# A retention head first, summed retention states, query decays by pieces, and work handed from VectorE to ScalarE in a fused hybrid block

## The chip, the cores and the metric

The kernel runs on one core of a Trainium2 chip. The metric is device time in microseconds (us) of one execution, lower is better. TensorE (PE in the profile) multiplies matrices, VectorE (DVE) and ScalarE (ACT) do the element-wise work, GpSimd (POOL) and SyncE (SP) mostly issue DMAs. Matrix products write to PSUM, whose banks DVE and ACT read.

## The reference

One block of a hybrid encoder over 1040 positions (16 meta tokens and 1024 inputs) of width 1024, in float32: a token mixer of four mLSTM heads and four retention heads, an output product, and a gated MLP with a causal convolution. Cut to what matters here:

```python
u = rmsnorm(h)                                   # (1040, 1024)
proj = u @ w_in                                  # q, k, v, o of 8 heads, and the gates' i, f columns
# heads 0..3, mLSTM
q, k = silu(causal_conv4(q)), silu(causal_conv4(k))
li = 15 * tanh(i / 15); lf = log_sigmoid(f)      # gates: decays between positions, from the data
h_ml = mlstm(q, k, v, li, lf)                    # state C = decay * C + k^T v, chunk by chunk
# heads 4..7, retention
q, k = rotary(q), rotary(k)                      # t1*cos - t2*sin, t1*sin + t2*cos on the two halves
h_rt = retention(q, k, v, log_gamma)             # the same state with a constant decay for each head
h += concat(sigmoid(o) * norm(h_ml), silu(g) * norm(h_rt)) @ w_out
a = causal_conv3(rmsnorm(h) @ w_up)
h += (silu(a) * (rmsnorm(h) @ w_gate)) @ w_down
out = rmsnorm(h)
```

## The kernel before

**Products.** Every product is made of three: each operand is split into a high part, rounded to a shorter format, and the low rest (`hi`, `lo`; L149 and L150 for the weights, `split` with L785 and L786 for the rest), and hi*hi, lo*hi and hi*lo are summed in PSUM (L374 to L376 for v, L384 to L386 for q, k and o, `mm3` L823 to L825 in the scan).

**Stages.** To about 38 us the input is normalised and v of the first head computed; `first_norm` gives the row scales `Rc` (positions on partitions) and `Rb` (positions along the row). Then q and k of the first head. Then the heads one after the other, some 83 us each, to about 700 us; the product with w_out to 865, the MLP's two halves to 1310 and 1545 us.

**A head.** The 1040 positions are 9 chunks, one of 16 and eight of 128. The three pieces 400, 384 and 256 wide are the groups of q, k and o. For head h the code writes, interleaved by `merge`: the six groups of o with chunks 0 to 3 of the scan; the nine groups of v of head h+1 with chunks 4 to 8 and the norms of the outputs (`post_steps`); `tables(h+1)`; the groups of q and k of head h+1. One chunk of the scan is `scan_a` (scores s, their decayed form pt, decayed keys kw, decayed queries qd) and `scan_b` (u = kw^T v, n = pt v + qd S, state C, its split S).

**mLSTM tables.** After q piece 0 of the first head, `gates()` computes decays of all four mLSTM heads with positions along the row, with small matmuls pg, pe, pf, pt in between, and writes them to the DRAM tensor `scr`. `tables(h)` loads for each head two tables spread over 128 partitions: A1 (decays within a chunk: mask added by L533, exponential by L536) and A2 (decays of queries). A1 is read by `scan_a` for pt (L803), A2 for qd (L810). Retention heads use A1 and A2 for the rotary cosines and sines instead.

**Order.** The Tile framework schedules the program: it takes the order of the code as a priority, simulates engines and queues, and sets one fixed order for each engine and each DMA queue. An engine executes its instructions in that order, so one that waits holds up all behind it; SP issues its DMAs in order too. PSUM is given out in tags: `pp` three banks, `sA` two, `num`, `upd` and `tr` one each. A PSUM bank is written again only when its readers are done.

**Other names.** `wsum` (L192, L194) prepares sums of blocks of w_out and w_down in DRAM by accumulating DMAs on POOL, one set per call of `wsum_next`. `gts` (L352) takes the gates' eight columns, which ride with v of the first head (264 columns instead of 256). `mx` (L908) is the gated, normed output, `sig` the activated o, `vl` (L350) the low part of v, whose reading frees the bank of pv.

Of the kernel before, what the change touches and what calls it, by code (L numbers as in the profile page):

```python
# [17 lines left out]
P = 128  # L18
# [21 lines left out]
R36 = NCH * H  # L40
PIECES = [(0, 400, (0, 1, 2, 3)), (400, 784, (4, 5, 6)), (784, 1040, (7, 8))]
# [12 lines left out]

V_MIX, V_FFN, V_FIN, V_MLG, V_RTG, V_CONV, V_FCONV, V_BI, V_BF = 0, 8, 16, 24, 32, 40, 72, 138, 139
V_N = 140
C_ID, C_M01, C_GV, C_GV0, C_EPS = 0, 128, 256, 260, 264
C_N = 268
# [3 lines left out]
def body(ctx, tc, h_in, vecs, cst, mask_in, rot, w_v0, w_v, w_fm, w_out, w_up, w_gate, w_down, out):  # L62
# [18 lines left out]
    cs = per.tile([P, C_N], F32, name="cs")  # L81
# [51 lines left out]
    def issue(upto):  # L133
        while issued[0] < min(upto, len(units)):
# [8 lines left out]
            sub = 2 if key[:2] == ("v", 0) else 1  # L143
# [18 lines left out]
    def u_v(h):  # L162
        for half in range(2):
            if h == 0:
                unit(("v", 0, half), w_v0[half], 4 * 264)
            else:
                unit(("v", h, half), w_v[h - 1, half], 4 * 256)
# [6 lines left out]
    def last_two(k, raw=None):  # L174
        raw = raw_tile(f"m{k}") if raw is None else raw
        nc.sync.dma_start(raw[:, :D], w_out[k])
        for t in range(2):
            if k:
# [27 lines left out]
    u_v(0)  # L206
    u_f(0, "q")
    u_f(0, "k")
    for h in range(8):
        u_f(h, "o")  # L210
        if h:
            u_m(h - 1)
        if h < 7:
            u_v(h + 1)
            u_f(h + 1, "q")
            u_f(h + 1, "k")
# [114 lines left out]
    Rg = st.tile([P, H, NCH], F32, name="Rg")  # L331
    ug = st.tile([P, KB, 32], F32, name="ug")
# [14 lines left out]
    def v_evac(h, c, L, src):  # L347
# [3 lines left out]
        if h == 0:  # L351
            nc.vector.tensor_scalar(gts[:L, :, c, :], src[:L, DV:DV + 8].rearrange("p (a b) -> p a b", a=2), Rc[:L, c:c + 1], None, ALU.mult)  # L352

    def v_group(h, c, tag="pp"):
        t0, L = CH[c]
        nv = 264 if h == 0 else 256
# [33 lines left out]
    def qk_group(h, kind, p):  # L390
# [7 lines left out]
        if h < H:  # L398
# [9 lines left out]
            nc.vector.tensor_scalar(cv[:, :n], raw[:, 3:3 + n], vec[:, w + 3:w + 4], None, ALU.mult)  # L408
            for j in (2, 1, 0):
                nc.vector.scalar_tensor_tensor(cv[:, :n], raw[:, j:j + n], vec[:, w + j:w + j + 1], cv[:, :n], ALU.mult, ALU.add)  # L410
            x = nc.scalar.activation(dst, cv[:, :n], AF.Silu)
            if h == 0 and kind == "q" and p == 0:
                after(x, last["sqrt"])
        else:
            nc.vector.tensor_tensor(raw[0:64, :n], pt[64:128, :n], A2[64:128, t0:t1], ALU.mult)
            nc.vector.tensor_tensor(raw[64:128, :n], pt[0:64, :n], A2[0:64, t0:t1], ALU.mult)
# [98 lines left out]

    def tables(h):
        if h > H:
            return
        if h == H:
            nc.sync.dma_start(A1, rot[:, 0])  # L520
            nc.sync.dma_start(A2, rot[:, 1])
            nc.vector.tensor_tensor(A2, A2, Rb, ALU.mult)
            nc.vector.tensor_tensor(A1, A1, Rb, ALU.mult)
# [253 lines left out]
    pre = {}  # L777
    state = {}
    outs = {}

    def split(src, n, nm, tag):
# [5 lines left out]
        return hi, lo  # L787

    def scan_a(h, c):
# [12 lines left out]
        if h < H:  # L802
            nc.vector.tensor_tensor(ptf[:, :L], s[:, :L], A1[:, t0:t0 + L], ALU.mult)  # L803
            if not last:
                w = cols[:, 1, c * H + h:c * H + h + 1]
                nc.scalar.activation(kh, s[:, P:2 * P], AF.Copy, scale=w)
                nc.vector.scalar_tensor_tensor(kl, s[:, P:2 * P], w, kh.bitcast(F32), ALU.mult, ALU.subtract)
# [149 lines left out]
    def first_norm(i):  # L957
# [11 lines left out]
        for f in evacs[i]:  # L969
            f()  # L970
# [37 lines left out]

# [576 lines left out]
```

## Time and profile before

| | |
|---|---|
| three runs | 1549.11, 1551.58, 1552.46 us; median 1551.58 |
| the profiled execution | 1551.16 us, its span 1549.4 us |
| PE busy | 1520.5 us, 98% of the span |
| DVE busy | 1085.4 us, 70% |
| ACT busy | 735.2 us, 47% |
| POOL busy | 90.5 us, 6% |
| DMA | 212.35 MB, 137 GB/s on average |

Matmuls overlap in the profile: one of 256 columns is shown with a duration of some 290 ns, yet the next starts 117 ns later; in full flow the start-to-start distance is 0.117 us for 256 columns and 0.175 us for 384. So busy time says little of PE's rate, and what is read are its waits (idle time before an instruction, and what released it) and the granted clock, which is 1.00 when PE runs at full speed. The page divides the span into 40 slices of 38.7 us; smaller windows are needed to see a clock that is halved for a few microseconds.

### The profile page before, as it was taken

To read this page: it belongs to the slowest core of one execution; us is meant where nothing else is said; L and a number is where in the kernel's file an instruction comes from. 1 tells how busy PE (TensorE), PEld (TensorE's weight loads), DVE (VectorE), ACT (ScalarE), POOL (GpSimd) and SP (SyncE) were. 2 spreads that over 40 slices of the span, in tenths; PEclk is the share of its full clock that TensorE was granted. 3 is DMA by queue.
4 is the path that set the end of the run, shared out by engine and by line. 5 is a ranking of instruction groups with operands and counts; after the bars stand their busy time and mean duration, and the time that the engine had idled before them with its cause. 6 is when DMAs were issued, how large, how long until landed. Compare 5 with 4: busy or idle time off the path is not lost.

```text
span 1549.4 us, 25346 instructions
## 1 busy us (share of the span) xinstructions
PE 1520.5 (98%) x9763; PEld 1398.9 (90%) x9763; DVE 1085.4 (70%) x2312; ACT 735.2 (47%) x1491; POOL 90.5 (6%) x107
## 2 busy tenths in 40 slices
PE   8989999999999999999999999999999999999997
PEld 8989999999999999997788998999999999888887
DVE  8756758686866565678867778766666666778657
ACT  7565555554242433435454455444444444434443
POOL 0110112112120210000000000000000000000000
PEclk9999999999999999999999999999999999999998
DMA  5676768778777773226542225332222224933213
GB/s 190 153 165 165 137 160 193 167 189 181 192 167 179 148 160 90 64 74 245 189 138 97 87 95 185 102 102 83 82 82 82 76 82 142 378 103 111 95 41 109
DMA packets 104904, 212.35 MB, mean 137 GB/s; under 512 B 9352, under 2 KB 31568, under 8 KB 104784
## 3 DMA queue, kind: packets, MB, share of 16 engines
q1 hardware_dynamic: 86096, 175.80, 33.9%
q0 software_dynamic: 18544, 34.87, 14.9%
q8 instruction: 76, 1.25, 0.3%
q14 instruction: 44, 0.36, 0.1%
q10 hardware_dynamic: 144, 0.07, 0.0%
HBM read 181.31 MB, written 84.19 MB: 171 GB/s over the span
## 4 chain that ended last, share of the span: by engine, by line
PE 93%; DMA 3%; DVE 2%; ACT 1%; SPq 0%; issue 0%; DVEq 0%; ACTq 0%
PE pv L374 4%; PE po L386 4%; PE po L384 4%; PE po L385 4%; PE pv L375 4%; PE pv L376 4%; PE pdx L554 3%; PE pdx L556 3%; PE pdx L555 3%; PE pup_x L555 2%; PE pup_x L556 2%; PE pga_x L554 2%; PE pga_x L556 2%; PE pga_x L555 2%; PE pup_x L554 2%; PE pk L384 2%
## 5 line engine op out<-in xcount | busy, mean ns | idle before, releaser
L374 PE MATMUL pv<-hi_v,uh 128*128 128x256 f32 (+1 forms) x512 | 148.4, 290 | 7.6 <-DVE sig L428 3.6
L375 PE MATMUL pv<-lo_v,uh 128*128 128x256 f32 (+1 forms) x512 | 147.6, 289 | 0.0
L376 PE MATMUL pv<-hi_v,ul 128*128 128x256 f32 (+1 forms) x512 | 145.8, 286 | 0.0
L384 PE MATMUL po<-uh,hi_o 128*128 128x386 f32 (+2 forms) x384 | 124.7, 325 | 0.0
L386 PE MATMUL po<-uh,lo_o 128*128 128x386 f32 (+2 forms) x384 | 122.6, 319 | 0.0
L385 PE MATMUL po<-ul,hi_o 128*128 128x386 f32 (+2 forms) x384 | 122.5, 319 | 0.0
L374 PEld LDWEIGHTS pv<-hi_v,uh 128*128 128x128 f32 x512 | 98.2, 192 | 11.6 <-DVE sig L428 3.8
L375 PEld LDWEIGHTS pv<-lo_v,uh 128*128 128x128 f32 x512 | 98.1, 192 | 0.8 <-DVE lo_v L150 0.8
L376 PEld LDWEIGHTS pv<-hi_v,ul 128*128 128x128 f32 x512 | 97.9, 192 | 0.0
L243 ACT CAST hi_up<-raw_up 128x512 fp32r<-128x512 f32 (+1 forms) x52 | 36.4, 719 | 106.7 <-PE pga_z L555 61.2
L384 PEld LDWEIGHTS po<-uh,hi_o 128*128 128x128 f32 x384 | 72.4, 188 | 0.2
L385 PEld LDWEIGHTS po<-ul,hi_o 128*128 128x128 f32 x384 | 72.4, 188 | 0.1
L386 PEld LDWEIGHTS po<-uh,lo_o 128*128 128x128 f32 x384 | 72.3, 188 | 0.0
L244 DVE TENSOR_TENSOR lo_ga<-fraw_ga,hi_ga 128x512 fp32r<-128x512 f32 (+1 forms) x52 | 41.8, 807 | 37.8 <-ACT hi_ga L243 37.6
L554 PE MATMUL pup_x<-uh_g,hi_up 128*128 128x256 f32 (+1 forms) x240 | 67.2, 282 | 0.4 <-ACT uh_g L1024 0.4
L555 PE MATMUL pup_x<-ul_g,hi_up 128*128 128x256 f32 (+1 forms) x240 | 67.4, 283 | 0.1
L244 DVE TENSOR_TENSOR lo_up<-raw_up,hi_up 128x512 fp32r<-128x512 f32 (+1 forms) x52 | 41.3, 808 | 36.0 <-ACT hi_up L243 35.2
L556 PE MATMUL pup_x<-uh_g,lo_up 128*128 128x256 f32 (+1 forms) x240 | 66.3, 282 | 0.0
L194 POOL DMA_DIRECT2D wsd<-w_down_d x55 | 50.9, 1026 | 262.8 <-DMA wsd<-w_down_d 166.1
L384 PE MATMUL pq<-uh,hi_q 128*128 128x400 f32 (+2 forms) x192 | 62.2, 324 | 3.7 <-DVE vl L350 2.5
L385 PE MATMUL pq<-ul,hi_q 128*128 128x400 f32 (+2 forms) x192 | 62.4, 325 | 0.0
L386 PE MATMUL pk<-uh,lo_k 128*128 128x400 f32 (+2 forms) x192 | 62.1, 324 | 0.0
(751 smaller groups left out, 5009.9 us busy)
## 6 DMA issues: line engine op xcount, KB each, us to landing
wsd<-w_down_d SPq DMA_DIRECT2D x22, 512.0 KB, 6.6
wsd<-w_down_d POOLq DMA_DIRECT2D x22, 512.0 KB, 6.5
raw_up<-w_up_d SPq DMA_DIRECT2D x22, 512.0 KB, 3.9
fraw_ga<-w_gate_d SPq DMA_DIRECT2D x22, 512.0 KB, 3.9
acts<-cv SPq DMA_DIRECT2D x44, 256.0 KB, 2.0
rd<-wsd SPq DMA_DIRECT2D x22, 512.0 KB, 3.3
wsd<-w_down_d POOLq DMA_DIRECT2D x33, 256.0 KB, 5.1
raw_o<-w_fm_d SPq DMA_DIRECT2D x16, 512.0 KB, 3.8
```

Source lines behind the costliest of these rows:

```text
L194: nc.gpsimd.dma_start(x, v, accum_op=ALU.add)
L243: nc.scalar.copy(hi[:, o:o + n], x)
L244: nc.vector.tensor_tensor(lo[:, o:o + n], x, hi[:, o:o + n].bitcast(F32), ALU.subtract)
L374: nc.tensor.matmul(pv[:L, :nv], a, hi[:, o:o + nv], start=kb == 0, stop=False)
L375: nc.tensor.matmul(pv[:L, :nv], a, lo[:, o:o + nv], start=False, stop=False)
L376: nc.tensor.matmul(pv[:L, :nv], b, hi[:, o:o + nv], start=False, stop=kb == KB - 1)
L384: nc.tensor.matmul(pt[:, :n], a, uh[kb][:, t0:t1], start=kb == 0, stop=False)
L385: nc.tensor.matmul(pt[:, :n], a, ul[kb][:, t0:t1], start=False, stop=False)
L386: nc.tensor.matmul(pt[:, :n], b, uh[kb][:, t0:t1], start=False, stop=kb == KB - 1)
L554: m.append(nc.tensor.matmul(pt, ah, xh_, start=first and k == 0, stop=False, skip_group_check=True))
L555: nc.tensor.matmul(pt, ah, xl_, start=False, stop=False, skip_group_check=True)
L556: m.append(nc.tensor.matmul(pt, al, xh_, start=False, stop=last and k == n - 1, skip_group_check=True))
```

## The change

It has seven parts.

1. **Order of the heads.** `ORDER = [4, 0, 1, 2, 3, 5, 6, 7]`: retention head 4 goes first, and the gates' columns ride with its v. `gates()` is written after all of the first head's q and k, no longer after q piece 0, and the mLSTM tables are first loaded for the second head in order. The rotary tables are loaded at the start (two DMAs, ahead of `raw_q` on SP) and again for head 5, since A1 and A2 are overwritten in between; their scaling by `Rb` goes by pieces (`rotary_norm`). The first head's o groups call no `wsum_next`. The first head's v scale `Rg` is computed inside `first_norm`.
2. **Summed states.** For heads 4, 5 and 6, u of all chunks accumulates in one PSUM bank, and S is split straight from it; the chunk's decay moves into the constant tables `gv` and `epsz` (new tile `gtab`), with one rescale in PSUM at chunk 4. The C instruction (L861, L865) goes for these heads. u of the next chunk now has to wait until both halves of S have been read from the bank. One DVE addition per output piece comes in for the epsilon of the norm, in all retention heads.
3. **Query decays by pieces.** mLSTM's qd is no longer computed for each of eight chunks (a product and a split each) but for three pieces, in place in A2, with the two halves in tiles of `accp`.
4. **Convolution tap.** The first of four taps, for each of the 24 groups of mLSTM's q and k, goes from DVE (L408) to ACT.
5. **Rotary moves.** The two half products (L415, L416), 64 partitions each, for the 24 groups of retention's q and k, become two ACT copies out of PSUM and one DVE product over 128 partitions.
6. **Gated output in place.** mx is written over sig, and the tile mx goes.
7. **Order of table loads.** A2's readers are done earlier because of part 3, so A2's load for the next head is issued apart from A1's.

The core of the diff:

```diff
+ORDER = [4, 0, 1, 2, 3, 5, 6, 7]
+HF = ORDER[0]
...
 def qk_group (h, kind, p)
-            nc.vector.tensor_scalar(cv[:, :n], raw[:, 3:3 + n], vec[:, w + 3:w + 4], None, ALU.mult)
+            nc.scalar.activation(cv[:, :n], raw[:, 3:3 + n], AF.Copy, scale=vec[:, w + 3:w + 4])
...
-            nc.vector.tensor_tensor(raw[0:64, :n], pt[64:128, :n], A2[64:128, t0:t1], ALU.mult)
-            nc.vector.tensor_tensor(raw[64:128, :n], pt[0:64, :n], A2[0:64, t0:t1], ALU.mult)
+            nc.scalar.copy(raw[0:64, :n], pt[64:128, :n])
+            nc.scalar.copy(raw[64:128, :n], pt[0:64, :n])
+            nc.vector.tensor_tensor(raw[:, :n], raw[:, :n], A2[:, t0:t1], ALU.mult)
             last["qk"] = nc.vector.tensor_tensor(dst, pt[:, :n], A1[:, t0:t1], ALU.mult)
             nc.vector.tensor_tensor(dst, dst, raw[:, :n], ALU.add)
...
+    def rotary_norm(t0, t1):
+        for a in (A2, A1):
+            nc.vector.tensor_tensor(a[:, t0:t1], a[:, t0:t1], Rb[:, t0:t1], ALU.mult)
...
+    def summed(h):
+        return H <= h < 7
...
 def scan_a
+            if c == max(chs[0], 1):
+                x = accp.tile([P, 2 * HB], F32R, tag=f"rr{p % 2}", name=f"qh{h}_{p}")
+                x = qds[h, p] = x[:, :p1 - p0], x[:, HB:HB + p1 - p0]
+                nc.vector.tensor_tensor(A2[:, p0:p1], qT[:, p0:p1], A2[:, p0:p1], ALU.mult)
+                nc.scalar.copy(x[0], A2[:, p0:p1])
+                nc.vector.tensor_tensor(x[1], A2[:, p0:p1], x[0].bitcast(F32), ALU.subtract)
             if c:
-                qf = wk.tile([P, P], F32, tag="qd", name=f"qd{h}_{c}", bufs=1)
-                nc.vector.tensor_tensor(qf, q, A2[:, t0:t0 + L], ALU.mult)
-                qd = split(qf, P, f"qd{h}_{c}", "qd")
+                qd = tuple(x[:, t0 - p0:t0 - p0 + L] for x in qds[h, p])
...
 def scan_b
-            up = pn[:, DV:] if one_bank else ps.tile([P, 512], F32, tag="upd", name=f"u{h}_{c}")
-            mm3(up[:, :nv], kw, v, True, True)
+            if summed(h):
+                if c == 0:
+                    state["up"] = ps.tile([P, 512], F32, tag="upd", name=f"u{h}")
+                up = state["up"]
+                if c == 4:
+                    nc.vector.tensor_scalar(up[:, :nv], up[:, :nv], float(np.exp(lg[h - H] * P * 4)), None, ALU.mult)
+            else:
+                up = pn[:, DV:] if one_bank else ps.tile([P, 512], F32, tag="upd", name=f"u{h}_{c}")
+            mm3(up[:, :nv], kw, v, not summed(h) or c == 0, True)
...
+        if c < NCH - 1 and summed(h):
+            state["S"] = split(up[:, :nv], nv, f"S{h}_{c}", "S")
...
 the program
+    tables(HF)
     for kind in "qk":
         for p in range(3):
-            qk_group(0, kind, p)
-            if kind == "q" and p == 0:
-                gates()
-    tables(0)
+            if kind == "q":
+                rotary_norm(*PIECES[p][:2])
+            qk_group(HF, kind, p)
...
+    gates()
+    for i, h in enumerate(ORDER):
-        merge([lambda b=b, p=p: (o_group(h, b, p), p == 1 and wsum_next()) for b in range(2) for p in range(3)],
+        merge([lambda b=b, p=p: (o_group(h, b, p), p == 1 and i and wsum_next()) for b in range(2) for p in range(3)],
```

Where instructions stand, at three places. The engines' rows are those of the two built programs, in the order in which each engine takes them; a name like `po0_1_1` is o of head 0, half 1, piece 1, and the last number of a name is a buffer.

DVE where the first mLSTM tables come in, in the first head's o groups, before: the mask add of A1 (L533, which waits for A1's DMA) stands between the query decays and the rest of the first scan chunks.

```order
L428 TENSOR_TENSOR sig_175<-po0_1_1_1145,Rb_111 128x384
L786 TENSOR_TENSOR qd0_1l_1043<-qd0_1_1040,qd0_1h_1042 128x128
L810 TENSOR_TENSOR qd0_2_1114<-qT_186,A2_185 128x128
L533 TENSOR_TENSOR A1_184<-A1_184,mask_183 128x1024
L532 TENSOR_TENSOR A1_184<-A1_184,mask_183 128x16
L861 COPY C0_0_1063<-u0_0_1054 128x258
L786 TENSOR_TENSOR qd0_2l_1117<-qd0_2_1114,qd0_2h_1116 128x128
L869 BN_STATS bn0_0_1069<-num0_0_1050 16x6
L803 TENSOR_TENSOR pt0_1_1033<-s0_1_1031,A1_184 128x128
```

And in the changed kernel, at the same place, with retention head 4 in its scan: L545 is the same mask add.

```order
L839 TENSOR_TENSOR kwl4_1_1010<-s4_1_1005,kwh4_1_1009 128x128
L376 TENSOR_TENSOR v0_0_1248<-pv0_0_1239,v0_0_1248 16x256
L799 TENSOR_TENSOR pt4_1l_1019<-pt4_1_1007,pt4_1h_1018 128x128
L545 TENSOR_TENSOR A1_185<-A1_185,mask_184 128x1024
L836 SCALAR_TENSOR_TENSOR pt4_2_1076<-s4_2_1074,cs_73 128x128
L799 TENSOR_TENSOR S4_0l_1035<-u4_1025,S4_0h_1034 128x256
L901 BN_STATS bn4_0_1038<-num4_0_1022 16x6
L358 SCALAR_TENSOR_TENSOR vl_190<-v0_0_1248,Rc_180,vh_189 16x256
L156 TENSOR_TENSOR lo_q_0_0_1236<-raw_q_0_0_1233,hi_q_0_0_1235 128x1024
```

Two scan chunks of head 4 have moved ahead of the mask add, the query decays are gone from there, and S4_0l, whose reading lets PE's u of chunk 1 begin, stands behind it. On PE, 104 matmuls stand from the gates' pf to that u, and pf itself stands 38 matmuls later than before.

SP's queue where the tables of head 2 (before) are loaded: L529 loads A2 and A1, L920 stores mx.

```order
L528 DMA A1_184<-scr_179 128x16
L146 DMA raw_q_2_0_2381<-w_fm_d 128x1024
L192 DMA wsw65_5_134<-w_out_d 256x1x512
L192 DMA wsw73_5_142<-w_out_d 256x1x512
L146 DMA raw_k_2_0_2884<-w_fm_d 128x1024
L146 DMA raw_o_2_0_2890<-w_fm_d 128x1024
L920 DMA mxd2_96<-mx1_0_0_2446 128x386
L920 DMA mxd3_97<-mx1_0_1_2454 128x386
L529 DMA A2_185<-scr_179 128x8x128
L529 DMA A1_184<-scr_179 128x8x128
```

The same in the changed kernel, for head 1 (L541 loads the tables):

```order
L540 DMA A1_185<-scr_179 128x16
L152 DMA raw_q_1_0_2281<-w_fm_d 128x1024
L198 DMA wsw65_3_132<-w_out_d 256x1x512
L198 DMA wsw73_3_140<-w_out_d 256x1x512
L541 DMA A2_186<-scr_179 128x8x128
L152 DMA raw_k_1_0_2758<-w_fm_d 128x1024
L152 DMA raw_o_1_0_2764<-w_fm_d 128x1024
L953 DMA mxd0_94<-sig_175 128x386
L953 DMA mxd1_95<-sig_175 128x386
L541 DMA A1_185<-scr_179 128x8x128
```

Four other loads and stores now stand between the loads of A2 and A1, which went back to back before.

DVE at the first head's q, before: L405 scales pq piece 0 and is the one reader of its bank.

```order
L405 TENSOR_TENSOR rq0_0_667<-pq0_0_642,Rb_111 128x400
L408 TENSOR_SCALAR cvq0_0_670<-rq0_0_667,vec_72 128x400
L403 COPY rq0_1_759<-rq0_0_667 128x3
L303 RECIPROCAL Rc_180<-Rc_180 128x3
L410 SCALAR_TENSOR_TENSOR cvq0_0_670<-rq0_0_667,vec_72,cvq0_0_670 128x400
L350 SCALAR_TENSOR_TENSOR vl_189<-pv0_4_392,Rc_180,vh_188 128x256
```

In the changed kernel (L423 waits for ACT's two copies out of the same bank, L424 reads the bank):

```order
L309 RECIPROCAL Rc_180<-Rc_180 128x3
L1007 TENSOR_TENSOR Rg_181<-Rc_180,gtab_182 128x3
L423 TENSOR_TENSOR rq4_0_670<-rq4_0_670,A2_186 128x400
L424 TENSOR_TENSOR qT_187<-pq4_0_645,A1_185 128x400
L358 SCALAR_TENSOR_TENSOR vl_190<-pv4_4_396,Rg_181,vh_189 128x256
L360 TENSOR_SCALAR gts_177<-pv4_4_396,Rc_180 128x2x4
```

The bank's last reader is now the fourth of these and stands behind a reciprocal, the new Rg and L423; pq piece 1 goes to the same bank in both programs.

116 lines of the change are left out of this document (67 added, 49 removed).

## The prediction

> **What bounds the kernel now.** First the page: its busy shares and the chain that ended last.
>
> ```profile
> PE 1520.5 (98%) x9763; PEld 1398.9 (90%) x9763; DVE 1085.4 (70%) x2312; ACT 735.2 (47%) x1491; POOL 90.5 (6%) x107
> PE 93%; DMA 3%; DVE 2%; ACT 1%; SPq 0%; issue 0%; DVEq 0%; ACTq 0%
> ```
>
> PE is the bound, and the change leaves PE its matmuls. Only two things can be won: PE's waits, and time at a lower clock. Work taken from DVE counts where PE waits for DVE, and nowhere else. So next the list of PE's waits (total, times, longest):
>
> ```profile
> PE pv L374 <- DVE sig L428: 3.6, 1, 3.6
> PE pq L384 <- DVE vl L350: 2.5, 1, 2.5
> ...
> PE pv L374 <- DVE vl L350: 1.9, 1, 1.9
> ...
> PE u L823 <- ACT pt_0h L785: 0.9, 1, 0.9
> ...
> PE n L823 <- ACT num L857: 0.8, 1, 0.8
> ...
> PE n L824 <- DVE S_5l L786: 0.4, 1, 0.4
> ```
>
> To see where they lie, and the clock there, windows of 20 us (busy time of PE, PEld, DVE, ACT, POOL; granted clock; DMA share), then of 2 us:
>
> ```profile
> 80.00:100.00 20.00, 15.57 (x116) 13.98 (x114) 6.05 (x21) 10.58 (x23) 1.64 (x2) 0.94 0.82 197
> 120.00:140.00 20.00, 17.33 (x118) 16.59 (x117) 11.33 (x30) 10.74 (x25) 0.51 (x1) 0.91 0.46 115
> 160.00:180.00 20.00, 20.00 (x135) 19.83 (x135) 13.12 (x33) 9.02 (x16) 5.51 (x6) 1.00 0.74 149
> 220.00:240.00 20.00, 17.48 (x115) 16.84 (x114) 11.56 (x27) 11.63 (x22) 1.07 (x1) 1.00 0.64 204
> 98.00:100.00 2.00, 1.03 (x4) 0.93 (x4) 1.12 (x6) 2.00 (x8) 0.00 (x0) 0.50 1.06 414
> 100.00:102.00 2.00, 1.92 (x9) 1.73 (x9) 1.22 (x5) 1.98 (x5) 0.50 (x1) 0.50 0.56 228
> 102.00:104.00 2.00, 2.00 (x11) 2.00 (x11) 1.02 (x3) 1.99 (x5) 0.57 (x1) 0.50 0.36 33
> 104.00:106.00 2.00, 2.00 (x17) 2.00 (x16) 1.94 (x4) 1.07 (x4) 0.00 (x0) 0.85 0.99 160
> 132.00:134.00 2.00, 2.00 (x11) 2.00 (x11) 1.49 (x6) 2.00 (x8) 0.00 (x0) 0.50 0.04 10
> 134.00:136.00 2.00, 2.00 (x13) 2.00 (x13) 0.80 (x3) 1.14 (x2) 0.00 (x0) 0.68 0.60 136
> ```
>
> After both stalls the clock is halved for a while. Busy time times one minus the clock gives what that cost: 0.5 + 1.0 + 1.0 + 0.3 = 2.8 us, and 1.0 + 0.6 = 1.6 us. Most other windows of the heads are full, like 160 to 180. What DVE did at the stalls, and the chain to the first:
>
> ```profile
> 95.75 1.23 DVE L533 TENSOR_TENSOR A<-A,mask 128x1024 f32<-128x1024 f32 x1 [3.30 <-DMA A<-scr]
> 129.83 1.23 DVE L533 TENSOR_TENSOR A<-A,mask 128x1024 f32<-128x1024 f32 x1 [2.38 <-DMA A<-scr]
> 225.79 1.23 DVE L533 TENSOR_TENSOR A<-A,mask 128x1024 f32<-128x1024 f32 x1 [6.80 <-DMA A<-scr]
> 310.17 1.23 DVE L533 TENSOR_TENSOR A<-A,mask 128x1024 f32<-128x1024 f32 x1 [4.45 <-DMA A<-scr]
> 75.87 0.34 PE pf L494 x2
> ...
> 77.69 1.28 ACT L506
> ...
> 79.70 4.70 DMA scr<-A
> ...
> 84.98 10.76 DMA A<-scr
> ```
>
> DVE stands at the mask add of A1 until its DMA lands, and the instructions that free PE's banks (sig, vl) stand behind. Of four such waits three reach PE; that of 4.45 us at 310 does not.
>
> **What the change can win.** Head 0's stretch, 80 to 140: waits 3.6 + 1.9 + 0.9 + 0.8 = 7.2 us and clock 2.8 + 1.6 = 4.4 us; head 2, at 226: 2.5 us, clock 1.00. Together 14.1 us.
>
> **Tables of heads 1 to 3.** A2 is free earlier, its load goes apart, and DVE waits for one load of A1 instead of two. A single one took 5.7 us here:
>
> ```profile
> 124.15 0.37 SPq L529 DMA_DIRECT2D A<-scr  x1
> ...
> A<-scr SPq DMA_DIRECT2D x2, 512.0 KB, 8.7
> ```
>
> (issued 124.15, landed by 129.83; the second row, for 84 to 97, is the median of the pair). Five DVE instructions, some 1.5 us, stand between A1's last reader and the mask add, so DVE would wait some 4 us at each of three heads, while PE has v of chunks 7 and 8 still to do. The 4.45 us at 310 was covered, 6.80 was not: I take 0 us, with 0 to 2 as bounds. So the 2.5 us are won.
>
> **First tables.** They now come during head 4's scan, where DVE still stands at the mask add, and u of chunk 1 needs S_0l behind it. PE reaches that u 104 matmuls after pf. Its pace there:
>
> ```profile
> 75.87:95.12 19.25, 18.39 (x137) 17.05 (x137) 5.16 (x18) 11.08 (x18) 3.57 (x4) 1.00 0.66 119
> ```
>
> 19.25 us less the wait of 0.9, over 137 matmuls: 0.134 us each, so 14.0 us after pf. A1 lands as the sum of: pf to the write, 3.8 us before (75.87 to 79.70), with a sigmoid and a table load (1.28) in it that may now be done ahead, so 1.9 to 3.8; the write, 4.7 us while wsum's accumulations held the DMA engines, which no longer start there, so 2.0 (a 256-KB store, below) to 4.7; issue 0.5; the loads 8.7 to 10.8. Sum 13.1 to 19.8. Behind it come the mask add 1.23, a pt of retention 0.28 and S_0l 0.41 (rows below), 1.9 us. So S_0l is ready 15.0 to 21.7 us after pf, and the stall is 1.0 to 7.7 us. I take 3.4 us, nearer the low end, as the accumulations are gone from this place, and with it 1.6 us of clock (0 to 2.8): 5.0 us.
>
> ```profile
> acts<-cv SPq DMA_DIRECT2D x44, 256.0 KB, 2.0
> ...
> 436.43 0.28 DVE L813 SCALAR_TENSOR_TENSOR pt<-s,cs 128x128 f32<-128x128 f32 x1
> ...
> L785 ACT CAST S_1h<-C x8: 407/408/411, 106.1 to 683.7; 128x258 fp32r<-128x258 f32 x4, 128x256 fp32r<-128x256 f32 x4
> L786 DVE TENSOR_TENSOR S_1l<-C,S_1h x8: 405/408/421, 107.6 to 685.3; 128x258 fp32r<-128x258 f32 x4, 128x256 fp32r<-128x256 f32 x4
> ```
>
> [...]
>
> The rows show half clock after two of three places with 2 to 4 us of waiting; the sum goes by them.
>
> **First head's q.** pq piece 1 takes the bank of piece 0:
>
> ```profile
> 42.35 0.57 DVE L405 TENSOR_TENSOR rq<-pq,Rb 128x400 f32<-128x400 f32 x1 [0.62 <-PE pq L386]
> 42.98 0.44 PE L384 MATMUL pq<-uh,hi_q 128*128 128x384 f32 x1 [0.18 <-DVE rq L405]
> 42.84 0.26 ACT L302 ACTIVATE Rc<-pca,epsc 128x3 f32<-128x3 f32 x1 [3.27 <-PE pca L296]
> 47.81 0.48 ACT L312 COPY Rb<-pra 128x384 f32<-128x384 f32 x1 [3.03 <-PE pra L308]
> ```
>
> Before, one DVE instruction freed it. Now ACT scales Rc (to 43.1), copies two halves (0.48 each, as Rb's copy, to 44.1), then DVE does two products of 0.57, to 45.3: 2.3 us later, with handoffs 2.5. Bounds: 0 (a copy ahead of Rc, as the two are independent, and later pieces have slack) to 4 (each piece lags again). I take 2.5, and 0.8 for the clock, half of 1.6. This moves all behind it, pf too, and so adds nothing to the first tables.
>
> **What DVE and ACT save or get.** Rows by form:
>
> ```profile
> L865 DVE SCALAR_TENSOR_TENSOR C<-C,u x26: 389/420/422, 437.2 to 698.7; 128x256 f32<-128x256 f32 x26
> L810 DVE TENSOR_TENSOR qd<-qT,A x32: 260/283/293, 91.2 to 382.0; 128x128 f32<-128x128 f32 x32
> L785 ACT CAST qd_1h<-qd x4: 298/300/308, 91.5 to 321.9; 128x128 fp32r<-128x128 f32 x4
> L408 DVE TENSOR_SCALAR cvq<-rq,vec x12: 347/418/429, 43.0 to 325.4; 128x400 f32<-128x400 f32 x4, 128x384 f32<-128x384 f32 x4, 128x256 f32<-128x256 f32 x4
> L415 DVE TENSOR_TENSOR rq<-pq,A x12: 425/559/577, 399.6 to 657.5; 64x400 f32<-64x400 f32 x4, 64x384 f32<-64x384 f32 x4, 64x256 f32<-64x256 f32 x4
> ```
>
> C goes for 24 chunks less 3 rescales: 21 x 0.42 = 8.8 us of DVE. The query decays: 32 x (0.28 + 0.28) of DVE and 32 x 0.30 of ACT become 12 triples of about three times the width; taken at 0.55 an instruction (L415's for 400 columns), 17.9 becomes 13.2 us on DVE. 24 taps of 0.42 go from DVE to ACT, 10.1 us. Of the rotary pairs 24 x 0.55 = 13 us goes from DVE, and 48 copies at up to 0.48 = 23 us come to ACT. All in all some 36 us off DVE and 28 us onto ACT (47% busy). From 160 to 700 us PE waited once, for the 2.5 us counted above; PE's own work covers the rest, so I cost all this at 0. If that cover is gone somewhere, one late copy costs up to its 0.5 us. The epsilon additions, mx in place and the later wsums are hidden by the same full PE: 0. So are the rotary tables at the start, two loads of half a megabyte ahead of raw_q on SP:
>
> ```profile
> 9.71 2.91 SPq L146 DMA_DIRECT2D raw_q<-w_fm_d  x1
> ...
> raw_q<-w_fm_d SPq DMA_DIRECT2D x1, 512.0 KB, 10.5
> ```
>
> Issued at 9.71 and landed at some 20 us, raw_q feeds a product that ends at 42.3; later by the loads' own 6 us, it still waits for PE.
>
> **Summed states.** u of the next chunk waits for S's second half instead of C: split 0.41 + 0.41 in place of 0.42, 0.4 us later, at 21 places. Before, n needed S just as much, only six matmuls (0.7 us) later on PE, and waited 0.4 us once in the program. So between 0 and 21 x 0.4 = 8.4; nearest to the row of one wait: 0.5 us.
>
> **Sum.** 14.1 - 5.0 - 2.5 - 0.8 - 0.5 = 5.3 us, against the profiled 1551.16: 1545.9 us. The median of the runs is 0.4 above that execution, which gives 1546.2 us.
>
> **The rivals.**
>
> *No wait is left.* The loads run at their quick ends (A1 at 13.1 us after pf) and the stall is 1 us without a clock loss: 14.1 - 1.0 - 2.5 - 0.5 = 10.1, so 1541.5 us, the clock of the first q left out too. For it: DMA is freer there. Against: A1 still needs two trips through DRAM, while PE has only 14 us of work.
>
> *The clock stays full.* Neither of the two new stalls lasts as long as the one before 98.97, and no half clock follows either, as none followed the 2.5 us at 226. Then the 1.6 and 0.8 us fall away: 1543.8 us. The halving at 132 speaks against it. [...]
>
> *The wait only moves.* The loads are no quicker than before (pair 10.8, write 4.7): stall 7 us, clock 2.8, with the first q's 3.3 and 0.5: 13.6 of 14.1 us are given back, 1551.1 us. For it: the mask add still stands ahead of the scan's work.
>
> *The summed state makes it slower.* Each of 21 u's stands right behind its S: ACT and DVE take the split in their own order, and PE is held 0.5 us (0.4, and a handoff) at each: 10.5 us instead of 0.5, net 4.7 us slower than before, 1556.3 us. From 0.3 us a place the gain is gone, from 0.4 it is slower by over 0.2%. For it: there is one bank for u, so nothing else can run ahead of the wait. Against: S was late once for n, by 0.4 us.
>
> **How the numbers follow.** The sum 0.42 (own range 1543.5 to 1548.4, from the first tables' 2 to 8 us), no wait left 0.14, clock full 0.10, moved 0.20, slower 0.14. 0.2%, 3.1 us, is about what a measurement of this kernel can tell from no change, so faster means below 1548.5. Faster: nearly all of the first three cases, 0.63; same: most of the fourth, 0.20; slower: the last and the fourth's tail, 0.17. The range goes from just under the best case to between the two worst ones, 1540 to 1554 us, which leaves out about 2 in 10.
>
> **What would show it.** In the profile after, between 80 and 140 us: a PE wait of 2 to 6 us for u or what follows it, released by S_0l, with DVE at L545 waiting for A1; none at 215 to 230 and 300 to 315. At 43 to 46 a wait of pq for DVE L424, some 2.5 us. Clock 1.00 in all but one or two windows up to 140. DVE some 36 us less busy, ACT 28 more. In heads 5 and 6 at most a microsecond of waits of u. The prediction is wrong if DVE stands at L545 for less than 1 us in the first head, if it waits over 5 us at a later head and PE with it, or if u waits at chunk after chunk in heads 4 to 6.

## The result, and the profile after

The changed kernel takes 1558.67 us (median of eight runs, 1557.17 to 1565.95) where the kernel before takes 1551.51 beside it (1547.80 to 1554.11): a ratio of 1.006, interval 1.004 to 1.008. It is slower by 0.6%, where 0.35% faster was forecast, and lies outside the range. The profiled execution has a span of 1557.0 us, against 1549.4 before.

The page of the changed kernel, busy shares and chain:

```profile
PE 1519.1 (98%) x9763; PEld 1395.1 (90%) x9763; DVE 1058.0 (68%) x2228; ACT 768.5 (49%) x1547; POOL 90.5 (6%) x107
PE 84%; DMA 5%; DVE 5%; ACT 4%; issue 1%; SPq 0%; DVEq 0%; ACTq 0%
```

PE does the same matmuls in the same busy time, so nothing was added to the bound. DVE has 27 us less and ACT 33 us more, as the change intends. But PE's share of the chain that ended last fell from 93% to 84%: more of the end is now set by DMA, DVE and ACT. The list of PE's waits (total, times, longest) says where:

```profile
PE tr L934 <- DVE sig L941: 3.9, 3, 1.7
PE n L846 <- ACT num L887: 3.5, 6, 1.6
PE u L846 <- ACT kwh L822: 3.1, 3, 1.1
PE pq L392 <- DVE gts L360: 2.9, 2, 1.6
PE u L846 <- DVE S_0l L799: 2.3, 1, 2.3
...
PE s L809 <- DVE kwl L839: 1.7, 1, 1.7
```

Before, single waits of 3.6, 2.5 and 1.9 us led this list (with one of 2.1 us at the start, which is the same in both). Now its first rows are sums of several waits of up to 1.7 us, and two of them are regular: the three of `tr` and the three of kwh come once for each of heads 1, 2 and 3.

To place the loss, take for each matmul its start less the time that the columns of all matmuls before it need at full pace (256 columns in 0.117 us), and see how much this lag grows over stretches with the same PE work in both kernels. This is worked out from all 9763 PE rows of each trace; a figure is good to about 0.5 us, as that much depends on where a stretch is cut.

| stretch (us in the changed kernel) | lag gained before | after | change forecast | change measured |
|---|---|---|---|---|
| start to first head's q and k, 0 to 56 | 12.5 | 15.6 | +3.3 | +3.1 |
| first head, next head's start, 56 to 213 | 20.2 | 15.9 | -6.6 | -4.3 |
| tables and scans of heads 1 to 3, 213 to 535 | 14.0 | 18.9 | -2.5 | **+4.9** |
| last heads and most of w_out, 535 to 829 | 12.9 | 14.3 | +0.5 | +1.4 |
| end of w_out, start of the MLP, 829 to 964 | 11.8 | 14.5 | 0 | +2.7 |
| rest | 5.5 | 5.4 | 0 | -0.1 |
| sum | 76.9 | 84.6 | -5.3 | +7.7 |

The sum is close to the 7.6 us between the two spans. The third row is the largest miss: 7.4 us off, of some 13 in all. In that stretch PE waited 7.4 us (3.9 for the gated output, 3.1 for kwh, 0.4 for num) where it waited 2.5 before; without these waits the two are alike (11.5 and 11.5).

Three groups of rows show how. DVE, then PE, in the changed kernel where head 1's tables come in (the timeline, us from the start):

```profile
216.46 0.43 DVE L799 TENSOR_TENSOR S_7l<-C,S_7h 128x258 fp32r<-128x258 f32 x1
221.49 1.22 DVE L545 TENSOR_TENSOR A<-A,mask 128x1024 f32<-128x1024 f32 x1 [4.60 <-DMA A<-scr]
222.63 0.61 DVE L941 SCALAR_TENSOR_TENSOR sig<-tr,vec,sig 128x384 f32<-128x384 f32 x1
...
221.60 0.34 PE L392 MATMUL pq<-uh,hi_q 128*128 128x400 f32 x1
223.29 0.55 PE L934 MATMUL tr<-cs,num 128*128 128x128 f32 x3 [1.34 <-DVE sig L941]
```

DVE stands at the mask add of A1 for 4.60 us until the DMA lands. Right behind it stands L941, the gated output, and this reads the one `tr` bank. PE's next transposes go into that bank, so PE stops at 221.9, some 5 us after DVE did at 216.9. The other two heads:

```profile
308.68 1.23 DVE L545 TENSOR_TENSOR A<-A,mask 128x1024 f32<-128x1024 f32 x1 [4.91 <-DMA A<-scr]
...
394.93 1.23 DVE L545 TENSOR_TENSOR A<-A,mask 128x1024 f32<-128x1024 f32 x1 [4.13 <-DMA A<-scr]
```

PE waited 1.66 us from 308.8 and 0.88 from 395.9. DVE's wait less PE's is 3.26, 3.25 and 3.25 us: that is how much a wait at this place is covered, in each of the three heads (the 5 us, less the mask add and L941 that DVE still has to do). The load itself took 7.0 us at head 1 (issued 214.52, DVE starts at 221.49).

The second regular wait: ACT in the changed kernel, ahead of head 1's own scan:

```profile
255.06 1.28 ACT L436 ACT_TABLE_LOAD   x1
256.36 0.53 ACT L436 ACTIVATE sig<-sig 128x386 f32<-128x386 f32 x1
256.90 1.28 ACT L419 ACT_TABLE_LOAD   x1
258.20 0.42 ACT L419 ACTIVATE kT<-cvk 128x256 f32<-128x256 f32 x1
258.63 1.28 ACT L436 ACT_TABLE_LOAD   x1
259.93 0.52 ACT L436 ACTIVATE sig<-sig 128x384 f32<-128x384 f32 x1
260.36 0.35 ACT L822 ACTIVATE kwh<-s,cols 128x128 fp32r<-128x128 f32 x1
```

The o groups' sigmoid (L436) and k's silu (L419) alternate, and each change loads a table, three times 1.28 us, ahead of kwh, for which PE's u waits 1.12 us at 260. The program has 59 table loads, before 55. Before, at the same place of head 1, one load separated the last silu (L411) from the sigmoids (L429), and PE had no such wait:

```profile
164.25 0.42 ACT L411 ACTIVATE kT<-cvk 128x256 f32<-128x256 f32 x1 [0.52 <-DVE cvk L410]
164.69 1.28 ACT L429 ACT_TABLE_LOAD   x1
166.81 0.53 ACT L429 ACTIVATE sig<-sig 128x386 f32<-128x386 f32 x1 [0.83 <-DVE sig L428]
```

Last, the first head. Windows of 20 us of the changed kernel (busy PE, PEld, DVE, ACT, POOL; granted clock; DMA share):

```profile
80.00:100.00 20.00, 19.64 (x151) 18.16 (x150) 6.92 (x24) 13.12 (x24) 0.00 (x0) 1.00 0.26 80
100.00:120.00 20.00, 16.35 (x133) 15.85 (x134) 12.47 (x40) 12.75 (x36) 3.96 (x4) 1.00 0.79 176
120.00:140.00 20.00, 18.20 (x133) 16.99 (x131) 10.24 (x29) 10.05 (x27) 1.87 (x2) 1.00 0.54 140
```

The half clock of before is gone from here: 1.00 in all three, where the windows of before showed 0.94 and 0.91.

### The profile page after: what moved, and what is told of

Read it like the earlier page. It is cut to its first block, busy times and chain, and to the rows that moved or that the text cites. A ratio compares the mean times of both kernels' runs of the same rounds, so it can differ in the third digit from the quotient of the medians.

```text
span 1557.0 us, 25337 instructions
## 1 busy us (share of the span) xinstructions
PE 1519.1 (98%) x9763; PEld 1395.1 (90%) x9763; DVE 1058.0 (68%) x2228; ACT 768.5 (49%) x1547; POOL 90.5 (6%) x107
## 4 chain that ended last, share of the span: by engine, by line
PE 84%; DMA 5%; DVE 5%; ACT 4%; issue 1%; SPq 0%; DVEq 0%; ACTq 0%
PE pv L382 3%; PE pv L383 3%; PE pv L384 3%; PE po L394 3%; PE po L393 3%; PE po L392 3%; PE pdx L566 3%; PE pdx L568 3%; PE pdx L567 3%; PE pup_x L567 2%; PE pup_x L568 2%; PE pga_x L566 2%; PE pga_x L568 2%; PE pga_x L567 2%; PE pup_x L566 2%; PE pdy L566 2%
## 5 line engine op out<-in xcount | busy, mean ns | idle before, releaser
L393 PE MATMUL pk<-ul,hi_k 128*128 128x400 f32 (+2 forms) x192 | 62.4, 325 | 0.0
L392 PE MATMUL pk<-uh,hi_k 128*128 128x400 f32 (+2 forms) x192 | 62.1, 324 | 0.0
```

What stands on the lines that cost most here:

```text
L392: nc.tensor.matmul(pt[:, :n], a, uh[kb][:, t0:t1], start=kb == 0, stop=False)
L393: nc.tensor.matmul(pt[:, :n], a, ul[kb][:, t0:t1], start=False, stop=False)
```

## The experiments

All ratios are against the kernel before, run beside it on the same chip; there it took 1553.1 to 1554.3 us. The changed kernel run again so took 1561.99, ratio 1.0052 (1.0032 to 1.0073), the number that those below are held against.

> The changed kernel itself, on the chip on which the versions of it ran. If its loss is a matter of its order of instructions, it is the same here: ratio 1.004 to 1.008. If part of the loss was chance of a chip or of the clock, 1.002 to 1.004, and the gains of the versions are to be counted from there.

### One part of the change undone at a time

**u_order**: the order of the heads, all else as changed.

```diff
-ORDER = [4, 0, 1, 2, 3, 5, 6, 7]
+ORDER = list(range(8))
```
(with `gates()` after q piece 0 and `tables(0)` after q and k, as before)

> The changed kernel with the heads in their old order 0 to 7: gates after q piece 0, tables of head 0 at the old place, rotary tables once; summed states, query decays by pieces, taps, rotary copies and mx in place stay. Theory A: the first q's loss (3.1 us) goes, the first tables' old loss comes back (some 10 us against 6 now), the mask add no longer has L941 right behind it at heads 1 to 3 (3.9 us less), the table loads on ACT are 55 instead of 59 (1 to 2 us less): 1554 to 1557 us. Rival B: no change, 1558.5 us. Rival C, the order of the heads makes the loss: 1551 us or less.

Measured: 1566.93 us, 1.0092 (1.0075 to 1.0110). Undoing the order makes it worse still. On DVE the mask add (3.88 us of waiting at 221) and then a norm's steps, which wait 3.42 us for ACT, stand ahead of `vl`; PE's pq waits for that 7.1 us at three places, longest 3.2, and pv waits 4.7 us in the first head. So the other parts, in the old order, are slower than the kernel before.

**u_qd**: the query decays by chunks again.

```diff
-nc.vector.tensor_tensor(A2[:, p0:p1], qT[:, p0:p1], A2[:, p0:p1], ALU.mult)
...
-qd = tuple(x[:, t0 - p0:t0 - p0 + L] for x in qds[h, p])
+nc.vector.tensor_tensor(qf, q, A2[:, t0:t0 + L], ALU.mult)
+qd = split(qf, P, f"qd{h}_{c}", "qd")
```

> The changed kernel, with the query decays again chunk by chunk (product and split for each of eight chunks), all else as changed. Theory A, engines held in order by the tables: in the changed kernel DVE stands at the mask add of A1 with the gated outputs (L941) right behind it, so PE waits 1.3, 1.7 and 0.9 us for the single bank of tr at heads 1 to 3, and the query decays by pieces are what brought L941 to that place; undone, vl comes first again and these 3.9 us go, while A2 and A1 go back to back and the mask add waits longer: 1554 to 1556 us. Rival B, the work moved to ACT (taps, copies) makes the loss: no change, 1558.5 us. Rival C, the order of the heads makes it: no change.

Measured: 1562.05 us, 1.0056 (1.0037 to 1.0075), no different. The wait that I had put down to the pieces stayed (row of PE's waits of this kernel):

```profile
PE tr L927 <- DVE sig L934: 5.3, 3, 2.6
```

So my first theory, that the query decays had moved the gated output behind the mask add, fell.

**u_tap**, **u_mx**: the tap on DVE again; a tile of its own for mx.

```diff
-nc.scalar.activation(cv[:, :n], raw[:, 3:3 + n], AF.Copy, scale=vec[:, w + 3:w + 4])
+nc.vector.tensor_scalar(cv[:, :n], raw[:, 3:3 + n], vec[:, w + 3:w + 4], None, ALU.mult)
```
```diff
-mx = sig(b, p)
+mx = mxp.tile([P, WMAX], F32, tag="mx", name=f"mx{h}_{p}_{b}", bufs=2)
```

> The changed kernel with the convolution tap w+3 on DVE again (24 instructions), all else as changed. Against before the changed kernel is at 1.006 and, with fewer table loads on ACT, at 1.001. Theory A, the order of sigmoid, silu and exponential on ACT holds up kwh and num: DVE is later with cvk by 0.42 us a piece, so silu of k falls further behind and the program has 65 table loads instead of 59: ratio 1.006 to 1.010. Theory B, ACT is held up by the taps themselves, which stand in its queue waiting for DVE's rk and rq (22 us of such waits between 130 and 470 us): ratio 1.000 to 1.003.

> The changed kernel with mx in a tile of its own again instead of in place in sig. The instructions of all engines stand in the same order as in the changed kernel. Theories A and B: sig is free again long before the next head's o needs it, so no change, ratio 1.004 to 1.008. Rival E, the stores of mx out of sig (two at a time, up to 4 us apart on SP) hold up the next sig and with it the banks of po: ratio 1.000 to 1.003.

Measured: 1558.73, 1.0035 (1.0022 to 1.0048), and 1559.99, 1.0039 (1.0024 to 1.0054). Both intervals overlap that of the changed kernel; neither part carries the loss, though a share of up to some 2 us is not excluded.

**u_nosum**: no summed states.

```diff
 def summed(h):
-    return H <= h < 7
+    return False
```

> The changed kernel with heads 4 to 6 keeping C in SBUF again (no summed states). Theories A and B: the loss lies in heads 0 to 3 and the first tables; u of chunk 1 of the first head still waits for A1's mask add through C or S, so no change within 0.2%: ratio 1.004 to 1.008. Rival F (the prediction's slower case), u waits for S chunk by chunk: ratio 1.000 to 1.003.

Measured: 1553.10, 0.9998 (0.9981 to 1.0015). That is 0.5% below the changed kernel, some 8 us, more than its profile shows: its span is 4.7 us shorter, and of the stretches in the table, 535 to 829 comes out 1.6 us better (12.7 for 14.3) and the end of w_out 3.7 (10.7 for 14.5), where no state is summed. Much of the 8 us is clock: the mean granted clock of its runs is 0.9948, where the changed kernel had 0.9926 and, run again, 0.9912, which is worth 3.4 to 5.6 us. Not the 10 us of the rival; how much of the rest belongs to this part stays open.

**u_rot**: the rotary halves as two DVE products again.

```diff
-nc.scalar.copy(raw[0:64, :n], pt[64:128, :n])
-nc.scalar.copy(raw[64:128, :n], pt[0:64, :n])
-nc.vector.tensor_tensor(raw[:, :n], raw[:, :n], A2[:, t0:t1], ALU.mult)
+nc.vector.tensor_tensor(raw[0:64, :n], pt[64:128, :n], A2[64:128, t0:t1], ALU.mult)
+nc.vector.tensor_tensor(raw[64:128, :n], pt[0:64, :n], A2[0:64, t0:t1], ALU.mult)
```

> The changed kernel with the rotary halves as two DVE products again instead of two ACT copies and one DVE product. Theory A: only the first head's q gains, where pq piece 1 waits for ACT's copies and DVE: up to 1 of the 3.1 us lost there; heads 5 to 7 had no PE waits: ratio 1.004 to 1.007. Theory B in its wider form, ACT's added work is what costs: ratio 1.000 to 1.003.

Measured: 1551.79, 0.9998 (0.9986 to 1.0010). The first stretch gains 13.1 instead of 15.6 us of lag: the 2.5 us of the first q are these copies. The waits of heads 1 to 3 stay (18.7 for 18.9 there). Here too the clock has a large share in the 8 us below the changed kernel: its mean over the runs is 0.9950.

### The suspected waits, taken away

**u_pool**: the mask add of A1 on GpSimd, so that DVE waits for no table.

```diff
-nc.vector.tensor_tensor(a, a, m..., ALU.add)
+nc.gpsimd.tensor_tensor(a, a, m..., ALU.add)
```

> The changed kernel, with the mask add of A1 on GpSimd instead of DVE, so that DVE never stands waiting for A1. Theory A: the wait of u for S_0l (2.3 us), of s for kwl (1.7) and of tr for L941 (3.9) go, 7.9 us; the add takes GpSimd some 2 us longer, which delays only A1's exponentials: 1550.5 to 1552.5 us. Rival B, ACT: 1558 us. Rival C, order: 1558 us. Rival D: A1 is late for the scan itself, and what does not wait at DVE waits at pt of the next head: 1556 to 1559 us.

Measured: 1568.96, 1.0092 (1.0073 to 1.0112), slower. The wait moved on (row of PE's waits):

```profile
PE n L846 <- ACT num L887: 18.4, 10, 4.4
```

ACT's exponentials of A1 now wait 14.6 us in all for this add (7.8 in the changed kernel), which takes 2.4 to 2.7 us on GpSimd and 1.2 on DVE, and the copy of n out of PSUM stands behind them. DVE was freed and ACT was held up instead.

**u_silu**: the first sigmoid of an mLSTM head's o after the last silu of its k. `after(x, y)` tells the scheduler to place x behind y.

```diff
+last["silu"] = nc.scalar.activation(dst, cv[:, :n], AF.Silu)
...
+if h < H and b == 0 and p == 0:
+    after(x, last["silu"])
```

> The changed kernel, with one order rule more: the first sigmoid of an mLSTM head's o comes on ACT after the last silu of its k, so that ACT does not load sigmoid, silu, sigmoid tables in turn (53 table loads in the program instead of 59). Theory A: PE's waits of u for kwh (1.1, 1.0, 0.95 us, at 259, 346 and 433) come from these loads (1.28 us each) ahead of kwh on ACT, and go, with two of n for num (0.2 each): 3.3 us less, 1555 us. Rival B, ACT is late because it has more to do altogether: the loads saved help by less than 1.5 us, 1557 to 1558.5 us. Rival C, order of the heads: no change.

Measured: 1556.10, 1.0013 (0.9996 to 1.0029), with 53 table loads instead of 59. The stretch of heads 1 to 3 gains 17.1 us instead of 18.9; one of the three waits for kwh is gone and two of 1.0 and 0.9 stay. The wait for `tr` stays (3.3 us).

**c_late**: the mask add of A1 behind the second gated output, that is behind the L941 which frees `tr` for piece 1.

```diff
+last["mix", p] = nc.vector.scalar_tensor_tensor(dst, tr..., vec..., sig..., ALU.mult, ALU.mult)
...
+x = nc.vector.tensor_tensor(a, a, m..., ALU.add)
+after(x, last["mix", 1])
```

> The changed kernel with one order rule more: the mask add of A1 comes on DVE after the second gated output of piece 1 of the head before (L941), so DVE does not stand in front of work that frees PE's banks while A1 is on its way; no instruction is added or taken away. Theory A, place in the queue: the waits for S_0l (2.3 us), kwl (1.7) and L941 (3.9) go, 7.9 us, less 1 to 2 for exponentials that come later on ACT: ratio 1.000 to 1.003 where the changed kernel has 1.006. Rival D, the table itself is late, as the mask add on GpSimd suggested (1.009): the wait turns up at ACT's exponentials or at pt, ratio 1.004 to 1.009.

Measured: 1554.65, 1.0002 (0.9986 to 1.0018). The waits of tr, S_0l and kwl are gone; 15.2 us in the stretch, where 18.9 were. New ones come on ACT: n for num, 2.49 us at 103, and u for pt_0h and kwh, 2.58 and 2.69 us at 176 and 263.

**c_rot_silu** is u_rot and u_silu together, **c_best** these two and c_late, **d_silu_late** is u_silu and c_late, with the rotary copies still on ACT.

> The changed kernel with the rotary halves on DVE again and the rule that the first sigmoid comes after the last silu. Theory A: the two gains are in different places (first q and first tables, some 4 us; table loads on ACT ahead of kwh, 2 to 3 us) and add up: ratio 0.997 to 0.999. Rival G, each undone part gains only because the planner lays out the rest anew: the gains do not add, ratio 0.999 to 1.002.

> The changed kernel with all three: rotary halves on DVE, first sigmoid after last silu, mask add after the gated output of piece 1. Theory A: 4 + 2.5 + 6 us off the changed kernel: ratio 0.996 to 0.993, faster than both. Rival D: the late mask add gives nothing or costs: ratio as with the first two alone, 0.997 to 1.002.

> The changed kernel with the two order rules (first sigmoid after last silu; mask add after the gated output) and the rotary copies still on ACT; c_best is this with the rotary halves on DVE and has 0.997. Theory A: the rotary copies cost the first q 2.5 us and little elsewhere, so 0.998 to 0.999. Rival G, gains of single edits do not add: 1.000 to 1.003.

Measured: 1548.34, 0.9973 (0.9956 to 0.9989); 1549.52, 0.9969 (0.9955 to 0.9983); 1552.08, 0.9995 (0.9981 to 1.0009). With both rules the stretch of heads 1 to 3 gains 11.4 us of lag (d_silu_late), near the 11.5 of before without its wait: the two account for that stretch. The third part, the rotary copies, is worth 0.26% between d_silu_late and c_best, measured on two chips and with intervals that just touch. But the gains don't add: c_rot_silu, without the late mask add, is as fast as c_best.

### Is it the order, or the place of the mask add?

**c_order**: the new order of heads and gates with the other parts undone (tap and rotary halves on DVE, query decays by chunks, no summed states; mx in place and the epsilon addition are kept).

```diff
+ORDER = [4, 0, 1, 2, 3, 5, 6, 7]
...
+gates()
+for i, h in enumerate(ORDER):
```
(against the kernel before)

> The kernel before with the new order of heads and gates alone (and mx in place, which did nothing by itself): taps and rotary halves on DVE, query decays by chunks, C for all heads. Theory A: the order takes away before's first stalls (some 10 us with the clock) and gives back 2 to 4 us at the first tables and the first q; without the other parts no L941 stands behind the mask add: ratio 0.995 to 0.998. Rival C, the order itself is what costs: ratio 1.003 to 1.008.

**d_order_late**: c_order with the two lines of c_late, and nothing else.

> The new order of heads and gates alone (as c_order), with the mask add of A1 on DVE after the second gated output of piece 1 of the head before. Theory A, the place of the mask add: the waits for S_0l and tr (4 to 5 us) go and the order gains what was forecast: ratio 0.997 to 1.000 where c_order has 1.0045. Theory C, the order itself: 1.003 to 1.005.

**d_before_late**: the kernel before with the same lines, for heads 1 to 3.

```diff
+if h:
+    after(x, last["mix", 1])
```

> The kernel before with the mask add of A1 for heads 1 to 3 after the second gated output of piece 1 of the head before; head 0's tables stay where they are. Theory A: the waits for vl at 130 and 226 (1.9 and 2.5 us) and the half clock after the first (1.6) go: ratio 0.996 to 0.998. Rival: the layout of the rest changes and gives it back, 0.999 to 1.003.

Measured: c_order 1560.17, 1.0045 (1.0029 to 1.0061). d_order_late 1545.63, **0.9956** (0.9936 to 0.9976). d_before_late 1548.89, 0.9971 (0.9958 to 0.9983). The order alone is as slow as the whole change, and one rule on one DVE instruction for each mLSTM head turns it into a gain of 0.44%; no other kernel here is faster, though its interval (of seven runs) overlaps those of c_best, c_rot_silu and d_before_late. By stretches of the table: c_order gains 19.4 us of lag from 56 to 213 and 17.0 from 213 to 535, d_order_late 14.0 and 14.1. Of the 14 us between the two, their profiled executions show 6.2; the mean granted clock of the runs, 0.9921 and 0.9944, is worth 3.6. (The scheduler lays out the rest anew with the rule, so other instructions move too: not all of the gain need come from the mask add.) DVE's rows at head 1's tables, first c_order, then d_order_late, where L544 is the mask add and L933 and L934 the gated output:

```profile
223.56 1.23 DVE L544 TENSOR_TENSOR A<-A,mask 128x1024 f32<-128x1024 f32 x1 [4.05 <-DMA A<-scr]
224.70 0.48 DVE L358 SCALAR_TENSOR_TENSOR vl<-pv,Rc,vh 128x256 fp32r<-128x256 f32 x1
225.09 0.61 DVE L933 SCALAR_TENSOR_TENSOR sig<-tr,vec,sig 128x384 f32<-128x384 f32 x1
```
```profile
220.38 0.62 DVE L934 SCALAR_TENSOR_TENSOR sig<-tr,vec,sig 128x384 f32<-128x384 f32 x1 [0.85 <-PE tr L927]
...
224.91 0.62 DVE L934 SCALAR_TENSOR_TENSOR sig<-tr,vec,sig 128x384 f32<-128x384 f32 x1 [0.95 <-PE tr L927]
225.44 1.22 DVE L544 TENSOR_TENSOR A<-A,mask 128x1024 f32<-128x1024 f32 x1
```

In the second the gated outputs no longer stand behind the mask add, and when DVE reaches it no wait for the table is shown. PE's waits in c_order:

```profile
PE u L838 <- DVE C L885: 3.6, 1, 3.6
PE tr L926 <- DVE sig L933: 2.8, 3, 1.5
```

and all over 1.5 us in d_order_late:

```profile
PE n L839 <- ACT num L880: 2.8, 3, 1.9
PE n L840 <- DVE S_6l L799: 2.2, 1, 2.2
PE pv L382 <- ACT hi_v L155: 1.7, 1, 1.7
PE pq L392 <- DVE gts L360: 1.6, 1, 1.6
```

Neither u for C nor tr is among them. Whether the new order is worth anything beyond the mask add is not settled: d_order_late and d_before_late differ by 0.15%, their intervals overlap, and at some 819 us their traces are about equally far ahead of the kernel before, by 5.6 and 4.9 us of lag.

## Why the prediction was wrong, step by step

**Tables of heads 1 to 3: the step that failed.** "DVE would wait some 4 us at each of three heads" was right (4.60, 4.91, 4.13), though the load took 7.0 us and not 5.7. "I take 0 us, with 0 to 2 as bounds" was not. I had taken the cover from one row of before, 4.45 us at 310, that did not reach PE, and from v's matmuls that PE still had to do. But the cover depends on which bank the instructions behind the wait free, and on how soon PE needs that bank again; both are set by the order, and the order was set anew. Before, at 310, a gated output (L908) stood behind the mask add too, but PE's next transposes into `tr` came 2.1 us after it had ended:

```profile
312.04 0.61 DVE L908 SCALAR_TENSOR_TENSOR mx<-tr,vec,sig 128x384 f32<-128x384 f32 x1
...
314.77 0.49 PE L901 MATMUL tr<-cs,num 128*128 128x128 f32 x3
```

In the changed kernel PE wants `tr` again some 5 us after DVE has stopped, not 9 us as there, and 3.25 us are covered. Cost: 3.9 us in the three heads, so that instead of 2.5 us won 1.4 were lost. DVE's order, which shows L941 behind the mask add, was there to be read before the run; I quoted it for the first head alone. My signs did not fit this either: I asked for a wait of DVE over 5 us at a later head, and 4.1 to 4.9 us were enough.

**"PE's own work covers the rest, so I cost all this at 0": failed too.** ACT's new order alternates silu and sigmoid, and its table loads hold up kwh, 3.1 us; u_silu takes a third of it away, u_silu with the late mask add all. Another 1.6 us come at 177, where DVE waits 4.51 us for the 16 meta columns of A1, ACT's exponential stands behind that, and num, which frees PE's n, behind both. I had counted how busy ACT was and not what it does in which order. Further waits of n for num before that cost 1.5 us; 0.75 of it is the wait of before at 129, which my 14.1 us counted as won and which is still there.

**First tables: right.** u of chunk 1 waits 2.33 us for S_0l, with DVE at the mask add for 4.17, and s 1.66 for kwl: 4.0 us against 3.4 of stall and 1.6 of clock. PE reached u 14.1 us after pf (14.0 forecast, by luck: 118 matmuls lie between in the trace and not 104, and they went faster), and A1 had landed 14.5 us after it (13.1 to 19.8). The clock of that place stayed at 1.00, so the 1.6 us of clock did not come. But it was luck: in c_late a wait hardly longer, 2.49 us at 103, stands in a window of 20 us that shows 0.91 (see the last section).

**First q: right in size.** 3.1 us against 2.5 and 0.8; u_rot shows that the copies carry 2.5 of it. It does not show as one wait for L424, but as a wait of 1.19 us for ACT's vh at 44.7 and one of 1.26 for DVE's gts at 51.2, ahead of the next pieces' products, and with the clock at 1.00.

**Summed states: the rival was wrong.** Between 434 and 706 us PE waited nowhere for more than 0.15 us, and the stretch of the last heads changed by 1.4 us in all (0.5 forecast); the 21 places cost nothing like 0.5 us each.

**Work moved: nearly right in size, and no gain.** DVE lost 27 us (36 forecast), ACT gained 33 (28). With d_silu_late at 0.9995 the parts that did this bring no time. They may even cost some: d_order_late, on the same chip, has the new order and the late mask add without them (and without the sigmoid rule) and is 0.4% faster, with intervals that do not meet; c_order and the changed kernel, without the rule, are level.

**Outside the sum: 2.7 us at the end of w_out.** Windows of 20 us, first before, then after:

```profile
820.00:840.00 20.00, 20.00 (x98) 16.74 (x97) 13.49 (x22) 10.17 (x22) 0.00 (x0) 0.91 0.32 113
840.00:860.00 20.00, 20.00 (x127) 17.71 (x126) 11.19 (x29) 5.61 (x17) 0.00 (x0) 1.00 0.21 72
```
```profile
820.00:840.00 20.00, 20.00 (x101) 16.94 (x99) 14.71 (x23) 8.47 (x18) 0.00 (x0) 0.96 0.17 52
840.00:860.00 20.00, 20.00 (x87) 16.08 (x87) 14.18 (x31) 10.06 (x25) 0.00 (x0) 0.86 0.36 132
```

The clock is halved there in both kernels, around a run of matmuls of one column, for 20 x 0.09 = 1.8 us before and 20 x (0.04 + 0.14) = 3.6 us after. In the 17 traces, before and after among them, the table's stretch from 829 to 964 gains 10.7 to 16.9 us of lag with the same code, and 16.9 in d_order_late, the fastest of all. Of the 2.7 us some 1.7 are one more half-clock period of 3.41 us, and I count it as chance; what sets it stays open.

## What to carry to other kernels

Cost an instruction that waits for a DMA by what stands behind it on its engine, which PSUM bank that frees and how soon PE needs the bank again, not by the engine's load; when a change lets a scheduler lay out the program anew, look up this place again in the new order, since a wait that was harmless before may now stand ahead of the one instruction that PE needs. What helped here was a rule that puts the wait behind the bank's readers (one rule: from 1.0045 to 0.9956, each against the kernel before beside it); giving the add to GpSimd did not, since ACT then waited and PE behind it. Undoing parts one at a time can mislead when each undoing sets a new order, and with it where the clock is halved: u_rot, u_nosum and c_late each came out level with the kernel before, yet c_rot_silu with the late mask add is no faster than without.

## What was not expected of the hardware

The length of a wait alone does not tell whether the clock is halved. It stayed at 1.00 after waits of 2.33 and 1.66 us at 99 to 107 in the changed kernel, but the windows of 20 us around three waits of 2.5 to 2.7 us in c_late show 0.91 to 0.96. The kernel before had no halving after its 2.5 us at 226. The two waits of 3.6 us, that of before (3.56 us, to 98.97) and this one of c_order, for C at 175, both saw the clock halved before they had ended, before from 97.75 on, c_order as follows (windows of 2 us):

```profile
174.00:176.00 2.00, 1.68 (x11) 1.36 (x9) 1.63 (x3) 1.97 (x3) 0.83 (x1) 1.00 1.14 197
176.00:178.00 2.00, 0.00 (x0) 0.00 (x0) 0.00 (x0) 1.97 (x4) 0.00 (x0) 1.00 0.84 100
178.00:180.00 2.00, 0.71 (x3) 0.74 (x4) 1.59 (x6) 1.08 (x4) 0.82 (x1) 0.51 0.44 73
180.00:182.00 2.00, 2.00 (x10) 2.00 (x9) 1.35 (x6) 1.40 (x5) 0.00 (x0) 0.50 0.70 115
182.00:184.00 2.00, 2.00 (x8) 2.00 (x8) 1.52 (x7) 0.45 (x2) 0.00 (x0) 0.50 0.08 13
```

And at the end of w_out the clock is halved while PE is busy throughout, around 32 matmuls of one column: before, these take 3.5 us from 830.78 on, and the clock is at 0.50 from 835.03 to 838.44; after, they take 4.3 us from 836.03 on, and the clock is at 0.50 from 838.60 to 845.43.

What sets the clock stays open here. Two places of before, side by side: PE was busy for 0.86 of the 3.41 us ahead of the half clock at 131.89, with waits of 0.75 and 1.92 us (first two rows), and for 2.32 and 1.98 us in the two rows that the 2.5 us at 226 fall into, where the clock stayed at 1.00 (last two):

```profile
128.48:131.89 3.41, 0.86 (x5) 0.66 (x6) 2.06 (x6) 2.96 (x8) 0.00 (x0) 1.00 0.28 96
131.89:135.30 3.41, 3.41 (x17) 3.41 (x18) 2.13 (x8) 2.85 (x9) 0.00 (x0) 0.50 0.20 59
224.05:227.46 3.41, 2.32 (x13) 1.98 (x11) 1.64 (x4) 0.41 (x2) 0.00 (x0) 1.00 0.54 105
227.46:230.87 3.41, 1.98 (x12) 1.91 (x13) 1.38 (x2) 3.41 (x10) 0.00 (x0) 1.00 0.32 98
```

The same kernel's times go with the clock: of the changed kernel's eight runs the two with a mean clock of 0.990 took 1565.76 and 1565.95 us, the two with 0.995 took 1557.17 and 1558.75.
